# A streaming-encoder block on one Trainium2 core: weight sums made from four loads and a step ahead, gates and boundary loads of the mixer moved by a product

## The chip, the cores and the metric

The kernel runs on one core of a Trainium2 chip. Its engines run side by side, each with its own queue of instructions: PE (TensorE: matmuls), DVE (VectorE: element work and scans), ACT (ScalarE: copies with conversion, activations), POOL (GpSimd, here mostly issuing stores) and SP (SyncE, issuing loads). The metric is the device time of one execution in microseconds (us), lower is better.

## The reference

The block works on x of 1024 rows by 1024 columns, in float32:

```python
x <- LN1(alpha*x + 0.5*FFN1(x))        # FFN(x) = (silu(x @ w_gate) * (x @ w_up)) @ w_down, 1024 -> 4096 -> 1024
z = x @ w_in[l]                        # q, k, v (512 columns each), lru input and its gate (512 each), 8 forget logits
x <- LN2(alpha*x + W_out [FoX(x) ; RG-LRU(x)])
x <- LN3(alpha*x + 0.5*FFN2(x))
```

FoX is causal attention with 8 heads of 64, whose scores get cumulated log-sigmoids of the forget logits. RG-LRU is a causal convolution over four steps, two sigmoid gates from 64 x 64 block matrices, and a linear recurrence along the rows; its result is multiplied by a gelu of the gate columns.

## The kernel before

**Operands.** Each float32 matmul is made of three on PE (`mm3`, L165 to L167): the operands are split into a high part (a cast to fp32r on ACT) and a low part (a subtraction on DVE), and hi x hi, lo x hi and hi x lo are added. Most large products are also done by a scheme that needs seven block products in place of eight (Strassen's, in Winograd's form): each operand is cut into four blocks "11", "12", "21", "22", and sums of blocks (for the weights "t1" to "t4") are operands too. Everywhere the seven products go in the order of `UNIT_ORDER`: "11", "21", "t2", "t1", "t3", "22", "t4". One product is 12 matmuls of 128 x 512.

**Stages.** In order of time: FFN1's gate and up products (to about 600 us), FFN1's down product, the mixer's input products `mixer_in`, `attention` (from about 1180 us), FFN2's gate and up (from about 1400 us), FFN2's down.

**FFN1's gate and up, and `prepare`.** `gate_up` goes through 16 pairs of column blocks, and each pair through a `Matrix` of gate and one of up, seven products each. Its own weights come as `raw`, and become operands by casts on ACT (L385) and subtractions on DVE (L386, L391). The results are copied by ACT (L690, L696, L700) and added by DVE (L703, L706); `silu` is L718. Beside this, `prepare` makes operands that are wanted later (of w_in, and the first ones of FFN2) and stores them to `wq_d`, `wv_d` and other DRAM tiles. It is a generator: `advance()` lets it do one step behind a product of a `Matrix`, 12 times a pair. It loads blocks of 128 x 256 ("aux", L276, by SP) into a pool of four buffers; `keep` (L282 cast on ACT, L283 low part on DVE, L284 store issued by POOL) makes one operand of a block, `less` (L287, DVE) subtracts two blocks in place, and `drop` gives up blocks and asks for as many new ones. A half unit is the seven operands of one half of the rows: it takes seven steps and, in the kernel before, six loads, since the blocks "22" and "12" come twice.

Between 150 and 200 us `mixer_consts` loads small constants and computes from them on ACT (L911, L912).

**The mixer.** `lru_and_qk(c)`, for c from 0 to 3, is one group of 128 channels of the recurrence: a `unit` of seven products for the LRU's input and gate columns, then a `unit` for q and k. A `unit` has two banks of PSUM's s part, `total` (products "11", "t2", "t3", "t4") and `z` ("t1", "22"), and an a bank for "21". What else is to be done stands in a table `then`, whose numbers 1 to 7 are the products it follows: convolution (L970, L972), `gates` (the split of u in L974, L975, two pairs of gate matmuls into a banks, then the recurrence L998 to L1010 and L1013), `out` (L1019 to L1022), `store` of q and k (L1227 on ACT, L1228 on DVE, stores by POOL). L1179 is the addition that is last to read `z`.

**Into attention.** In the last unit, `load_first` asks for head 0's q, kh and kl, `load_rows` for four rows of W_out, and `split_row` splits one (L157 on ACT, L158 on DVE); three more splits come behind the unit. In `attention`, `load` asks for the other operands of a head; `probs` makes the scores of 128 rows (L1329, L1330 on PE into an s tile, L1335 on DVE, L1336 on ACT), and `piece` a tile of the recurrence's part of the output product, with the splits of W_out.

**What sets the order.** A tile scheduler puts out each engine's queue: it follows the order of the program as priorities, the dependences between tiles, the buffers of the pools and `issue_after`. So a changed line can move other instructions too.

Of the kernel before, what the change touches and what calls it, by code (L numbers as in the profile page):

```python
# [13 lines left out]
ALU = mybir.AluOpType  # L14
# [47 lines left out]
class Block:  # L62
# [202 lines left out]
    def prepare(self, jobs, wsp, ap):  # L265
# [20 lines left out]
        def less(x, y):  # L286
            v.tensor_tensor(x, x, y, ALU.subtract)  # L287
# [10 lines left out]
        for blocks, to in jobs:  # L298
# [757 lines left out]
    def load_qk(self, h):  # L1056

        nc, b = self.nc, h % 2
        mine = slice(64 * b, 64 * b + 64)
        for j in range(2):  # L1060
            rows = slice(64 * j, 64 * j + 64)
            for n, src in (("q", self.q_d[h // 2, j]), ("kh", self.k_d[h // 2, 0]), ("kl", self.k_d[h // 2, 1])):
                self.row_load = nc.sync.dma_start(f32(self.heads[n][rows, b, :]), src[mine, :])

    def mixer_in(self, w_out, vw, vp, wp):
# [7 lines left out]
        with self.tc.tile_pool(name="lru_t", bufs=1, reuse_waits="tile") as tp, \  # L1073
# [80 lines left out]
            def unit(c0, c1, c3, then):  # L1154

                def done(n):
                    for g in then.get(n, []):
                        g()

                total = self.s_tile()[:, 0, :]  # L1160
                product(total, "11")
                nc.scalar.copy(c0, total)
                done(1)
                two = self.a_tile()
                product(two, "12")
                v.tensor_tensor(c0, two, c0, ALU.add)
                done(2)
                product(total, "s2", False)
                nc.scalar.copy(c1, total)
                done(3)  # L1170
                z = self.s_tile()[:, 0, :]
                product(z, "s1")
                nc.scalar.copy(c3, z)
                done(4)
                product(total, "s3", False)
                v.tensor_tensor(c3, total, c3, ALU.add)
                done(5)
                product(z, "s4", False)
                v.tensor_tensor(c1, z, c1, ALU.add)  # L1179
                done(6)  # L1180
                product(total, "22", False)
                then[7](total)
# [4 lines left out]
            def lru_and_qk(c, lru_then, qk_then):  # L1187
# [30 lines left out]
                then = {2: [first_conv], 4: [lambda: gates(0)], 6: [lambda: self.gelu_twice(g[:, 0, :], tmp), lambda: out(0)], 7: second_conv}  # L1218
# [5 lines left out]
                def store(n, half, src):  # L1224
# [11 lines left out]
                unit(r[:, 0, :], r[:, 1, :], r[:, 2, :], then)  # L1236
# [27 lines left out]
            w_rows = []  # L1264

            def load_first():
# [362 lines left out]
```

## Time and profile before

| | us |
|---|---|
| median of three runs | 2334.14 (2330.5 to 2335.61) |
| the profiled execution: its own time | 2331.18 |
| the profiled execution: its span | 2329.2 |
| busy in the span: PE / DVE / ACT / POOL | 2290.3 / 1704.9 / 1063.3 / 310.3 |

A busy PE is not PE at its peak: matmuls overlap, so that one row of 0.39 us follows another after 0.23 us. How much PE gets done in a stretch is therefore seen best in the number of its matmuls, and a slower clock in the distance from one start to the next. In a row of a timeline the columns are start, duration, engine, line, operation, out<-in, shapes, and in brackets the idle time before it with what ended it.

### The profile page before, as it was taken

To read this page: it belongs to the slowest core of one execution; us is meant where nothing else is said; L and a number is where in the kernel's file an instruction comes from. 1 tells how busy PE (TensorE), PEld (TensorE's weight loads), DVE (VectorE), ACT (ScalarE), POOL (GpSimd) and SP (SyncE) were. 2 spreads that over 40 slices of the span, in tenths; PEclk is the share of its full clock that TensorE was granted. 3 is DMA by queue.
4 is the path that set the end of the run, shared out by engine and by line. 5 is a ranking of instruction groups with operands and counts; after the bars stand their busy time and mean duration, and the time that the engine had idled before them with its cause. 6 is when DMAs were issued, how large, how long until landed. Compare 5 with 4: busy or idle time off the path is not lost.

```text
span 2329.2 us, 29518 instructions
## 1 busy us (share of the span) xinstructions
PE 2290.3 (98%) x10609; PEld 1896.2 (81%) x10609; DVE 1704.9 (73%) x2745; ACT 1063.3 (46%) x1767; POOL 310.3 (13%) x505
## 2 busy tenths in 40 slices
PE   9999999999999999999989999999999999999998
PEld 7878878787888888988778888888888888888887
DVE  8867777777558779876767999565656565577886
ACT  6444444444334335354556855434343333344342
POOL 0142223232100001111124210000000000000000
PEclk9999999999999999999999999999999999999999
DMA  4565666666276443457676844232323232564542
GB/s 154 195 213 197 222 208 228 208 215 214 105 263 242 140 146 139 152 177 243 211 246 202 241 149 141 86 118 86 118 89 124 94 119 86 188 245 172 181 143 73
DMA packets 221201, 394.44 MB, mean 169 GB/s; under 512 B 14256, under 2 KB 123120, under 8 KB 221056
## 3 DMA queue, kind: packets, MB, share of 16 engines
q1 hardware_dynamic: 184352, 268.50, 35.9%
q0 software_dynamic: 36704, 124.07, 13.6%
q8 instruction: 83, 1.36, 0.2%
q14 instruction: 62, 0.51, 0.1%
HBM read 264.56 MB, written 127.96 MB: 169 GB/s over the span
## 4 chain that ended last, share of the span: by engine, by line
PE 72%; issue 7%; DVE 3%; ACT 2%; DMA 2%; POOL 1%; DVEq 0%; POOLq 0%; ACTq 0%; SPq 0%
PE x L167 6%; PE x L165 6%; PE x L166 6%; PE a L166 6%; PE a L167 6%; PE a L165 6%; PE b L165 5%; PE b L166 5%; PE b L167 5%; PE s L166 5%; PE s L167 5%; PE s L165 5%; PE a L1371 1%; PE a L1350 1%; POOL wq_d L284 1%
## 5 line engine op out<-in xcount | busy, mean ns | idle before, releaser
L385 ACT CAST ws<-t 128x512 fp32r<-128x512 f32 x240 | 147.7, 622 | 311.7 <-PE b L166 139.4
L386 DVE TENSOR_TENSOR ws<-t,ws 128x512 fp32r<-128x512 f32 x240 | 164.2, 686 | 59.5 <-ACT ws L385 35.5
L165 PE MATMUL x<-As,ws 128*128 128x512 f32 x504 | 197.7, 392 | 5.0 <-ACT row L696 4.7
L165 PE MATMUL b<-As,ws 128*128 128x512 f32 x512 | 199.8, 390 | 0.7 <-ACT As L421 0.5
L166 PE MATMUL a<-ws,ws 128*128 128x512 f32 x512 | 199.7, 390 | 0.6 <-DVE ws L817 0.6
L165 PE MATMUL a<-ws,ws 128*128 128x512 f32 x512 | 199.2, 390 | 0.4 <-ACT row L709 0.4
L167 PE MATMUL a<-ws,ws 128*128 128x512 f32 x512 | 199.4, 389 | 0.0
L166 PE MATMUL b<-As,ws 128*128 128x512 f32 x512 | 199.4, 389 | 0.0
L167 PE MATMUL b<-As,ws 128*128 128x512 f32 x512 | 199.2, 389 | 0.0
L167 PE MATMUL x<-A,ws 128*128 128x512 f32 x496 | 194.4, 392 | 4.9 <-DVE ws L386 4.7
L167 PE MATMUL x<-As,ws 128*128 128x512 f32 x504 | 197.1, 391 | 0.0
L166 PE MATMUL x<-As,ws 128*128 128x512 f32 x504 | 197.0, 391 | 0.0
L165 PE MATMUL x<-A,ws 128*128 128x512 f32 x496 | 194.3, 392 | 2.0 <-ACT ws L385 1.2
L166 PE MATMUL x<-A,ws 128*128 128x512 f32 x496 | 193.1, 389 | 0.0
L814 ACT CAST ws<-raw 128x1024 fp32r<-128x1024 f32 x112 | 117.5, 1050 | 160.9 <-PE a L166 82.3
L385 ACT CAST ws<-raw 128x512 fp32r<-128x512 f32 x180 | 110.4, 621 | 172.5 <-PE x L166 136.2
L386 DVE TENSOR_TENSOR ws<-raw,ws 128x512 fp32r<-128x512 f32 x180 | 123.1, 687 | 85.2 <-ACT ws L385 74.3
L744 POOL DMA_DIRECT2D h_d<-row x96 | 69.5, 725 | 858.1 <-DVE row L738 846.0
L817 DVE TENSOR_TENSOR ws<-raw,ws 128x1024 fp32r<-128x1024 f32 x112 | 136.6, 1220 | 47.2 <-ACT ws L814 46.7
L165 PE MATMUL s<-ws,ws 128*128 128x512 f32 x384 | 149.5, 389 | 0.0
L167 PE MATMUL s<-ws,ws 128*128 128x512 f32 x384 | 149.4, 389 | 0.0
L166 PE MATMUL s<-ws,ws 128*128 128x512 f32 x384 | 149.4, 389 | 0.0
(326 smaller groups left out, 5421.7 us busy)
## 6 DMA issues: line engine op xcount, KB each, us to landing
raw<-h_d SPq DMA_DIRECT2D x56, 1024.0 KB, 5.4
h_d<-row POOLq DMA_DIRECT2D x96, 512.0 KB, 3.5
wd<-in_ffn_w_down_dram SPq DMA_DIRECT2D x32, 1024.0 KB, 7.6
raw<-in_ffn_w_gate_dram SPq DMA_DIRECT2D x30, 1024.0 KB, 5.2
raw<-in_ffn_w_up_dram SPq DMA_DIRECT2D x30, 1024.0 KB, 5.2
wq_d<-ws POOLq DMA_DIRECT2D x112, 256.0 KB, 3.8
wq<-wq_d SPq DMA_DIRECT2D x56, 512.0 KB, 4.1
aux<-in_w_in_dram SPq DMA_DIRECT2D x112, 128.0 KB, 3.3
```

What stands on the lines that cost most here:

```text
L165: mm(out, ah, bh, start=first, stop=False, skip_group_check=goes_on)
L166: mm(out, ah, bl, start=False, stop=False, skip_group_check=goes_on)
L167: mm(out, al, bh, start=False, stop=last, skip_group_check=goes_on)
L284: nc.gpsimd.dma_start(to, f32(t).rearrange("p l k f -> p l (k f)"))
L385: nc.scalar.copy(hi, src)
L386: v.tensor_tensor(lo, src, f32(hi), ALU.subtract)
L744: nc.gpsimd.dma_start(d[:, 2 * n:2 * n + 2], t.rearrange("p (r t) -> p r t", r=2))
L814: cast = nc.scalar.copy(hi, src)
L817: self.mark = v.tensor_tensor(lo, src, f32(hi), ALU.subtract)
L1350: nc.tensor.transpose(pa[:, (j % 4) * P:(j % 4 + 1) * P], p[:, j * P:(j + 1) * P], self.ident)
L1371: mm(pv[:, ps], vt[:, j, :], pts[h, qt][j // 4][l][:, j % 4, ps], start=j == 0 and l == 0, stop=j == last and l == 1)
```

## The change

`prepare` loads four blocks for a half unit instead of six and keeps all four until they have been used: `less` gets a place for its result, and every sum is made a step before it is kept, in the place of a block that is done with. The order in which operands are kept becomes 11, t1, 22, t3, t2, 21, t4 (before: 11, t1, 22, t2, 21, t4, t3); each still goes to its own place in DRAM.

In `unit` the seven steps get the names of `UNIT_ORDER`, and so do the tables `then`. The gates of the first half come after "t3" (before: after the product with s1, "t1"), those of the second half after "t2" (before: after "21"). The last unit has `total` in an a bank instead of an s bank. Head 0's q and kh are asked for behind "11" and kl and the cumulated sums behind "21" of the last unit, where before q, kh and kl came behind "21" and the sums in `attention`. Other heads' loads go by operand: q twice, kh twice, kl twice, then the sums.

```diff
-        def less(x, y):
-            v.tensor_tensor(x, x, y, ALU.subtract)
+        def less(to, x, y):
+            v.tensor_tensor(to, x, y, ALU.subtract)
...
-            a, b = ready[0:2]
+            a, b, c, d = ready
             keep(to["11"], a)
-            less(b, a)
-            drop()
+            less(a, b, a)
             yield
-            keep(to["t1"], b)
+            keep(to["t1"], a)
             yield
-            c = ready[1]
             keep(to["22"], c)
-            less(c, b)
-            drop()
+            less(b, c, b)
+            yield
+            keep(to["t3"], b)
+            less(c, c, a)
+            drop(2)
             yield
             keep(to["t2"], c)
             yield
-            a = ready[1]
-            keep(to["21"], a)
-            less(a, c)
+            keep(to["21"], d)
+            less(d, d, c)
             drop()
             yield
-            keep(to["t4"], a)
+            keep(to["t4"], d)
             drop()
-            a, b = ready[0:2]
-            less(a, b)
-            yield
-            keep(to["t3"], a)
-            drop(2)
             yield
...
-            blocks = [view[:, k, c] for k, c in ((up, c0), (up, c1), (down, c1), (down, c0), (down, c1), (up, c1))]
+            blocks = [view[:, k, c] for k, c in ((up, c0), (up, c1), (down, c1), (down, c0))]
...
-                total = self.s_tile()[:, 0, :]
+                total = self.a_tile() if last else self.s_tile()[:, 0, :]
...
-                then = {2: [first_conv], 4: [lambda: gates(0)], 6: [lambda: self.gelu_twice(g[:, 0, :], tmp), lambda: out(0)], 7: second_conv}
+                then = {"21": [first_conv], "t3": [lambda: gates(0)], "22": [lambda: self.gelu_twice(g[:, 0, :], tmp), lambda: out(0)], "t4": second_conv}
...
-                then = {2: [lambda: store(0, 0, r[:, 0, :]), lambda: gates(1), lambda: out(1)], 5: [lambda: store(1, 1, r[:, 2, :])],
-                        6: [lambda: store(1, 0, r[:, 1, :])], 7: lambda total: store(0, 1, total)}
+                then = {"21": [lambda: store(0, 0, r[:, 0, :])], "t2": [lambda: gates(1), lambda: out(1)], "t3": [lambda: store(1, 1, r[:, 2, :])],
+                        "22": [lambda: store(1, 0, r[:, 1, :])], "t4": lambda total: store(0, 1, total)}
...
+            def open_heads(names, k):
+                for l, n in enumerate(names):
+                    self.heads[n] = vp.tile([P, 2, T], F32 if n == "cum" else F32R, tag=f"w{k + l}", name=self.nm(n))
                 with self.tc.issue_after(self.row_load.ins):
-                    self.load_qk(0)
+                    for n in names:
+                        self.load_head(0, n)
...
-                           {3: [self.forget]} if c == 0 else {2: [load_first], 3: [load_rows], 6: [split_row]} if c == 3 else {})
+                           {"t2": [self.forget]} if c == 0 else
+                           {"11": [lambda: open_heads(("q", "kh"), 0)], "21": [lambda: open_heads(("kl", "cum"), 2)], "t2": [load_rows], "22": [split_row]} if c == 3 else {})
```

How the queues move is seen in the order of the instructions. In the kernel with the change the lines up to some 1050 are 5 lower (L381 is L386 before, L698 is L703, L906 and L907 are L911 and L912, L685 is L690, L704 is L709), those of `attention` 14 higher.

DVE, a half unit of `prepare` and the beginning of the next pair (`aux` is a block or a sum of blocks, `ws` a kept operand), before:

```order
L283 TENSOR_TENSOR ws_548_2719<-aux_541_2662,ws_548_2719 128x256
L287 TENSOR_TENSOR aux_543_2681<-aux_543_2681,aux_541_2662 128x256
L283 TENSOR_TENSOR ws_551_2755<-aux_543_2681,ws_551_2755 128x256
L283 TENSOR_TENSOR ws_552_2772<-aux_545_2701,ws_552_2772 128x256
L287 TENSOR_TENSOR aux_545_2701<-aux_545_2701,aux_543_2681 128x256
L283 TENSOR_TENSOR ws_555_2793<-aux_545_2701,ws_555_2793 128x256
L283 TENSOR_TENSOR ws_556_2810<-aux_546_2703,ws_556_2810 128x256
L287 TENSOR_TENSOR aux_546_2703<-aux_546_2703,aux_545_2701 128x256
L283 TENSOR_TENSOR ws_558_2830<-aux_546_2703,ws_558_2830 128x256
L703 TENSOR_TENSOR row_493_2485<-x_547_2705,row_492_2484 128x512
L287 TENSOR_TENSOR aux_549_2724<-aux_549_2724,aux_553_2777 128x256
L386 TENSOR_TENSOR ws_568_2846<-raw_566_2843,ws_567_2845 128x512
```

and now:

```order
L283 TENSOR_TENSOR ws_534_2691<-aux_525_2616,ws_534_2691 128x256
L287 TENSOR_TENSOR aux_525_2616<-aux_526_2618,aux_525_2616 128x256
L283 TENSOR_TENSOR ws_536_2725<-aux_525_2616,ws_536_2725 128x256
L287 TENSOR_TENSOR aux_526_2618<-aux_530_2656,aux_526_2618 128x256
L283 TENSOR_TENSOR ws_537_2742<-aux_530_2656,ws_537_2742 128x256
L287 TENSOR_TENSOR aux_530_2656<-aux_530_2656,aux_525_2616 128x256
L283 TENSOR_TENSOR ws_539_2761<-aux_526_2618,ws_539_2761 128x256
L283 TENSOR_TENSOR ws_542_2783<-aux_530_2656,ws_542_2783 128x256
L283 TENSOR_TENSOR ws_543_2800<-aux_532_2675,ws_543_2800 128x256
L287 TENSOR_TENSOR aux_532_2675<-aux_532_2675,aux_530_2656 128x256
L381 TENSOR_TENSOR ws_553_2816<-raw_551_2813,ws_552_2815 128x512
L698 TENSOR_TENSOR row_480_2459<-x_533_2677,row_479_2458 128x512
```

The sum with a reloaded block (L287 with aux_549 and aux_553) is gone from ahead of the next pair's first low part, and that low part (L386, now L381) has gone ahead of the addition L703 (now L698).

ACT around the mixer's constants (`lp` and `vecs` are the constants, `x` a product's bank), before:

```order
L282 CAST ws_313_1452<-aux_262_1313 128x256
L911 ACTIVATE lp_315_1497<-vecs_1488 128x4
L690 COPY row_272_1360<-x_329_1628 128x512
L912 ACT_TABLE_LOAD
L912 ACTIVATE lp_315_1497<-lp_315_1497 128x4
L282 CAST ws_320_1546<-aux_264_1332 128x256
```

and now:

```order
L906 ACTIVATE lp_312_1491<-vecs_1482 128x4
L282 CAST ws_311_1448<-aux_258_1291 128x256
L907 ACT_TABLE_LOAD
L907 ACTIVATE lp_312_1491<-lp_312_1491 128x4
L685 COPY row_270_1356<-x_326_1622 128x512
L282 CAST ws_317_1540<-aux_258_1291 128x256
```

The copy of a product (L690, now L685) stood ahead of the table load and now stands behind it and behind one more cast.

PE from the mixer into attention (`s` and `a` are banks, `wq` the last unit's operands, `w` the splits of W_out, `mix` the recurrence's output), before:

```order
L166 MATMUL s_1808_10134<-xT_1542_8210,wq_1828_10232 128x512
L167 MATMUL s_1808_10134<-xT_1541_8209,wq_1828_10232 128x512
L1329 MATMUL s_1855_10364<-kh_1821_10201,q_1820_10200 128x512
L1330 MATMUL s_1855_10364<-kl_1822_10202,q_1820_10200 128x512
L1329 MATMUL s_1855_10364<-kh_1821_10201,q_1820_10200 128x384
L1330 MATMUL s_1855_10364<-kl_1822_10202,q_1820_10200 128x384
L165 MATMUL a_1858_10378<-w_1833_10285,mix_1596_8869 128x512
```

and now:

```order
L1343 MATMUL s_1815_10284<-kh_1771_10071,q_1770_10070 128x512
L1344 MATMUL s_1815_10284<-kl_1776_10098,q_1770_10070 128x512
L1343 MATMUL s_1815_10284<-kh_1771_10071,q_1770_10070 128x384
L1344 MATMUL s_1815_10284<-kl_1776_10098,q_1770_10070 128x384
L165 MATMUL a_1818_10298<-w_1793_10206,mix_1556_8789 128x512
L166 MATMUL a_1818_10298<-w_1794_10207,mix_1556_8789 128x512
L167 MATMUL a_1818_10298<-w_1793_10206,mix_1557_8790 128x512
L165 MATMUL a_1818_10298<-w_1797_10228,mix_1620_9180 128x512
L165 MATMUL a_1768_10054<-xT_1501_8129,wq_1788_10153 128x512
```

The last product (from `xT`) stood ahead of the second scores; now the second scores and the first four matmuls of a piece, which read splits of W_out, stand ahead of it.

More of the change, by code (lines that the diff above doesn't have):

```diff
@@ L1152, in product, with unit, one, two @@
                     self.mm3(x, (w[:, 0, k, :], w[:, 1, k, :]), x_op(name, k), new and k == 0, k == 3, not new)
[L1154 to L1158, printed above, removed]
-                total = self.s_tile()[:, 0, :]
[L1161 to L1182, printed above, removed]
+            def unit(c0, c1, c3, then, last=False):
+                total = self.a_tile() if last else self.s_tile()[:, 0, :]
+                bank = {}
+                def one():
+                    product(total, "11")
+                    nc.scalar.copy(c0, total)
+                def two():
+                    x = self.a_tile()
+                    product(x, "12")
+                    v.tensor_tensor(c0, x, c0, ALU.add)
+                def six():
+                    product(total, "s2", False)
+                    nc.scalar.copy(c1, total)
+                def five():
+                    bank["z"] = self.s_tile()[:, 0, :]
+                    product(bank["z"], "s1")
+                    nc.scalar.copy(c3, bank["z"])
+                def seven():
+                    product(total, "s3", False)
+                    v.tensor_tensor(c3, total, c3, ALU.add)
+                def three():
+                    product(bank["z"], "s4", False)
+                    v.tensor_tensor(c1, bank["z"], c1, ALU.add)
+                def four():
+                    product(total, "22", False)
+                steps = {"11": one, "21": two, "t2": six, "t1": five, "t3": seven, "22": three, "t4": four}
+                for n in UNIT_ORDER:
+                    steps[n]()
+                    if n == "t4":
+                        then[n](total)
+                    else:
+                        for g in then.get(n, []):
+                            g()
@@ L1262, in s4 @@
                     parts("s4", j, quarters(j)[0][1])
[L1264 to L1268 removed]
+            w_rows, self.heads = [], {}
+            def open_heads(names, k):
+                for l, n in enumerate(names):
+                    self.heads[n] = vp.tile([P, 2, T], F32 if n == "cum" else F32R, tag=f"w{k + l}", name=self.nm(n))
                 with self.tc.issue_after(self.row_load.ins):
[L1270 removed]
+                    for n in names:
+                        self.load_head(0, n)
             def load_rows():
```

28 lines of the change are left out of this document (15 added, 13 removed).

## The prediction

> **What bounds the kernel now.** I read the page first, then a table by stage, the waits of PE, and the timeline around the longest of them.
>
> ```profile
> span 2329.2 us, 29518 instructions
> PE 2290.3 (98%) x10609; PEld 1896.2 (81%) x10609; DVE 1704.9 (73%) x2745; ACT 1063.3 (46%) x1767; POOL 310.3 (13%) x505
> ```
>
> PE is busy 98% of the span, and the change takes no matmul away. So all it can win are PE's stops and the slow matmuls after them. Busy time hides the second kind; counts of matmuls in a window (the first bracket behind its length) show both:
>
> ```profile
> 150.00:200.00 50.00, 46.28 (x191) 37.38 (x190) 37.40 (x83) 23.37 (x43) 21.51 (x34) 0.93 0.61 195
> 200.00:600.00 400.00, 393.19 (x1714) 319.76 (x1713) 301.45 (x543) 190.67 (x368) 111.81 (x161) 1.00 0.63 214
> 1050.00:1150.00 100.00, 97.75 (x425) 78.94 (x424) 68.27 (x111) 49.95 (x74) 15.27 (x26) 1.00 0.71 232
> 1150.00:1200.00 50.00, 43.06 (x168) 34.04 (x167) 33.77 (x50) 28.52 (x39) 8.26 (x14) 0.90 0.84 281
> 1500.00:1900.00 400.00, 400.00 (x1767) 331.20 (x1766) 247.87 (x366) 155.17 (x253) 27.26 (x40) 1.00 0.29 102
> ```
>
> The last row, FFN2 without stops, gives the full pace: 400 / 1767 = 0.2264 us a matmul. Against it 200 to 600 (FFN1 gate/up) is short of 53 matmuls, 12.0 us; 150 to 200 (the mixer's constants) of 30, 6.8 us; 1050 to 1150 (most of the mixer) of 17, 3.8 us; 1150 to 1200 (mixer into attention) of 53, 12.0 us. PE's waits name the stops:
>
> ```profile
> PE x L167 <- DVE ws L386: 4.7, 9, 1.0
> PE x L165 <- ACT row L696: 4.7, 2, 3.5
> PE s L1329 <- DVE ev L1228: 3.1, 1, 3.1
> PE s L1329 <- DVE raw L1179: 3.0, 1, 3.0
> PE a L165 <- ACT ua L974: 2.2, 5, 0.5
> PE a L166 <- DVE ue L975: 2.0, 5, 0.8
> ```
>
> Row 1 is the FFN1 pairs' boundaries, row 2 the constants (3.5) and one boundary, rows 3 and 4 the step into attention, rows 5 and 6 the gates: ten stops, 4.2 us. The change touches all four places.
>
> **Part 1: four loads and an earlier order in prepare.** One boundary, and the group that paces it (groups of 200 to 600):
>
> ```profile
> 294.67 0.41 ACT L282 CAST ws<-aux 128x256 fp32r<-128x256 f32 x1 [1.02 <-issue]
> 294.98 1.14 ACT L385 CAST ws<-raw 128x512 fp32r<-128x512 f32 x2
> 295.45 0.68 DVE L703 TENSOR_TENSOR row<-x,row 128x512 f32<-128x512 f32 x1
> 296.60 1.29 DVE L386 TENSOR_TENSOR ws<-raw,ws 128x512 fp32r<-128x512 f32 x2
> 297.34 0.50 PE L167 MATMUL x<-A,ws 128*128 128x512 f32 x1 [0.95 <-DVE ws L386]
> 409.48 0.50 PE L165 MATMUL x<-As,ws 128*128 128x512 f32 x1 [1.26 <-ACT row L696]
> L287 DVE TENSOR_TENSOR aux<-aux,aux 128x256 f32<-128x256 f32 x67 | 28.2, 424 | 26.5 <-DMA aux<-in_w_in_dram 20.3 <-DMA aux<-in_ffn_w_gate_dram 4.7 <-DMA aux<-in_ffn_w_up_dram 0.2
> ```
>
> DVE idles 25.2 us ahead of L287 for reloaded blocks; the half unit then ends late, its last cast (294.67) stands ahead of the next pair's first (294.98), and L386 comes 0.95 us late, behind L703 as well. In the change each block is asked for at least four steps before its sum, and a difference that is kept was made a step earlier. The order also puts L386 ahead of L703 (0.68). The seven casts, seven low parts, four differences and seven stores of a half unit stay; two of its six loads go, 40 of 128 KB in all, so nothing is added on any engine. At a boundary L386 comes 0.68 earlier by the order and up to 1.0 earlier by the cast that was late, against stops of 0.4 to 1.0. I take 9 of 12.0 us: some boundaries also wait for L385's own input. Bounds: 2 (only L703's place counts at the nine stops, and a later step of the chain is late instead) and 12.0.
>
> **Part 2: the constants.** Their DMAs are untouched, but the order of ACT around them moves.
>
> ```profile
> 160.37 0.21 ACT L911 ACTIVATE lp<-vecs 128x4 f32<-128x4 f32 x1 [4.45 <-DMA vecs<-in_lru_lambda_dram]
> 160.48 0.57 ACT L690 COPY row<-x 128x512 f32<-128x512 f32 x1
> 161.07 1.28 ACT L912 ACT_TABLE_LOAD   x1
> 169.06 0.71 ACT L282 CAST ws<-aux 128x256 fp32r<-128x256 f32 x2 [2.43 <-DVE aux L287]
> 170.30 0.79 PE L165 MATMUL x<-As,ws 128*128 128x512 f32 x1 [3.45 <-ACT row L696]
> 170.90 0.63 PE L166 MATMUL x<-As,ws 128*128 128x512 f32 x1
> 171.32 0.63 PE L167 MATMUL x<-As,ws 128*128 128x512 f32 x1
> ```
>
> Before, the copy that PE waits for (L690) comes right behind L911, and PE stops 0.26 us there; the large stop, 3.45, is at L696, where an L282 waits 2.43 us for L287. Behind that stop matmuls follow at 0.42 us (170.90 to 171.32) instead of 0.2264. Now L690's copy stands behind one L282 (0.4) and L912's table load and activation: 0.4 + 1.28 + 0.21 = 1.9 us more, so the first stop becomes about 2.2. The second loses most of the 2.43 that the L282 waited and keeps casts ahead of it: about 1.4 at full pace, none if PE was slow in between. The slow stretch now costs 6.8 - 3.45 - 0.26 = 3.1. With one stretch behind the first stop and no second stop: 2.2 + 3.1 = 5.3, to which I add 0.2 for half a chance of a rest of the second: 5.5, a gain of 1.3. With no slow stretch 2.2 + 1.4 = 3.6, a gain of 3.2; with one behind both stops, 9.8, a loss of 3.
>
> **Part 3: gates a product later.**
>
> ```profile
> 1168.05 0.51 PE L166 MATMUL a<-ue,hi 128*128 128x512 f32 x1 [0.33 <-DVE ue L975]
> 1168.82 0.69 ACT L998 ACTIVATE t<-a,vecs 128x512 f32<-128x512 f32 x1 [0.76 <-PE a L167]
> ```
>
> A product is 12 matmuls, 2.72 us. The first half's gates get it whole, and their stops (one of five pairs, 1.1 us) go. The second half's (eight of ten stops) stand behind the first half's recurrence, which starts with L998 when the first half's gates are done, 2.72 later too. So the distance between the halves stays, and of a second pair's stops I take off about a third, for the rows of the unit's stores that no longer stand between. Stops cost 4.2 plus some 0.17 each in the restart (at 409.48 PE is 1.42 behind its pace for 1.26 of idle), 5.9 in all; I take 2.4, between 0 and 5.9.
>
> **Part 4: into attention.** Timeline, PE first, then DVE and ACT:
>
> ```profile
> 1178.59 0.39 PE L167 MATMUL s<-As,wq 128*128 128x512 f32 x1
> 1181.93 0.50 PE L1329 MATMUL s<-kh,q 128*128 128x512 f32 x1 [2.95 <-DVE raw L1179]
> 1190.57 0.80 PE L1329 MATMUL s<-kh,q 128*128 128x512 f32 x1 [3.11 <-DVE ev L1228]
> 1197.03 0.40 PE L1329 MATMUL s<-kh,q 128*128 128x512 f32 x1
> 1181.19 0.68 DVE L1179 TENSOR_TENSOR raw<-s,raw 128x512 f32<-128x512 f32 x1
> 1185.11 4.80 DVE L158 TENSOR_TENSOR w<-wout,w 128x1024 fp32r<-128x1024 f32 x4
> 1189.84 0.68 DVE L1228 SCALAR_TENSOR_TENSOR ev<-s,ev 128x512 fp32r<-128x512 f32 x1
> 1190.44 1.21 DVE L1335 CUSTOM_DVE_ANT_0 p<-s,cum 128x1024 f32<-128x1024 f32 x1
> 1181.91 0.63 ACT L1227 ACTIVATE ev<-raw 128x512 fp32r<-128x512 f32 x1 [1.36 <-DVE raw L1179]
> 1182.44 3.88 ACT L157 CAST w<-wout 128x1024 fp32r<-128x1024 f32 x4
> ```
>
> Two banks hold `total` and `z` and are freed late: z by L1179 at 1181.87 (stop A), total by the last L1228 at 1190.52, behind the four L158 (stop B).
> Stop A stays. The bank that total leaves now takes the first scores; the second scores wait for z. From L998's start (1168.82) z comes free in 13.05 us, for 10.0 of which PE has work (to 1178.82). In the change PE has 43 matmuls behind the first of the second half's gates (three of the other gate, 36 of three products, four of scores), 9.74 us, and DVE has one L1228 (0.6 from start to start) less ahead of z: 12.4 - 9.7 = 2.7, a gain of 0.3.
> Stop B changes its cause. From z's release to the third scores it is now 1197.03 - 1181.87 = 15.2 us. In the change: L1227 0.63, the first L157 about 1.0, the first L158 1.2, together 2.8, the first piece's four matmuls to 3.7, the last product 2.72, to 6.4; L1227 0.6 and L1228 0.7, by then past the four L158 (0.63 + 1.0 + 4.8 = 6.4), L1335 1.21, 0.2 to start: 9.1. At half pace the product takes 1.4 more, 10.5. Gain 4.7 (slow) to 6.1; I take the slow end, since 2.95 of idle is followed by a slow stretch and 2.7 is nearer to that than to 1.26 (409.48, no slow row behind it). With stop A: 5.0.
> Price of the earlier loads: head 0's q, kh and then kl, cum are now asked for after the last unit's first two products.
>
> ```profile
> kh<-k_d SPq DMA_DIRECT2D x16, 256.0 KB, 6.0
> ```
>
> Asked for behind the first product, 2.7 to 5 us into the unit, kh lands at 11 at the latest, and the first scores, 54 matmuls into the unit, want it at 12.2: about 1.2 in hand, so nothing is charged. If kh were 2 late, PE would stop for 1 more.
>
> **Sum.** 9 + 1.3 + 2.4 + 5.0 = 17.7 us off the profiled execution, 2331.18 (its span of 2329.2 and 2.0 around it): 2313.5. The median of the three runs, 2334.14, is 3.0 above it, so on the scale of the median 2316.5; I predict **2316 us**.
>
> A rule bears on the largest doubt. The Trainium skill, "TensorE: Matmul & The Clock Gate", section "HAM oscillation", says that PE must not idle for more than about 3.4 us if its clock is to stay up. This trace differs: the slow stretch begins behind 2.95 of idle. By the page neither the 2.2 nor the 2.7 us stop would have one.
>
> **Rivals.**
> - *The clock stays up* at stops of 2.2 to 2.7. For: 1.26 has no slow stretch. Against: 2.95 has. Part 2 gives 3.2 and part 4 6.4, with 9 and 2.4: 21.0 off, 2313 on the scale of the median.
> - *All boundary and gate stops vanish*: 12.0 and 5.9 instead of 9 and 2.4, 24.2 off, 2310. For: each stop is under 1.3, and a product is 2.72. Against: DVE's order behind the recurrence.
> - *The boundaries stay*: the chain cast, subtraction, cast of the next sum is itself what paces a half unit, not the load; only 2 of 9 is won, 10.7 off, 2323.4. For: L282 waits for L287 (2.43 at 169.06). Against: 25.2 us of idle on DVE name the DMA.
> - *It does nothing*: the loads in flight are four deep as before, and another transfer is late at the same boundaries; the gains at attention are eaten by kh. 2334.
> - *Slower: z comes late at every channel group.* With the gates 2.72 later, the recurrence of the second half ends later, and the z bank of the next group's first unit is freed behind it. PE has about 1.2 us in hand there by my count of matmuls against DVE's chain; it decides once the chain slips by 4.2 (1.2 and a stop of 2.95). Then each of three group boundaries costs a stop and a slow stretch like stop A's, about 6: 18, against 10.3 of parts 1 and 2: 7.7 slower, 2342. For: at the last group stop A is this. Against: DVE is busy 68 of 100 us between 1050 and 1150, and a slip of one product leaves 1.5 missing.
>
> **How the numbers follow.** Forecast 0.48, clock up 0.13, all stops gone 0.10, boundaries stay 0.12, nothing 0.07, slower 0.10. A difference under 0.2% (4.7 us) can't be told from none. Faster: 0.48 + 0.13 + 0.10 + 0.12 = 0.83; same 0.07; slower 0.10. The forecast's own range is 2311 to 2322, from the bounds of parts 2 to 4; with the rivals on the fast side and the boundaries that stay, 2306 to 2327, which leaves out the last two cases.
>
> **What would show it.** Part 1: 200 to 600 with about 1755 matmuls, L287's idle for DMA near 0. Part 2: a stop of about 2.2 at L690's line and none of 3.45. Part 3: no first-half gate stop, second-half ones under 0.8. Part 4: a stop near 2.7 for z, then one for L158's first result, and third scores about 10 us after z's release. Wrong would be: stops at the starts of units in the mixer, or PE waiting for kh or q.

## The result and the profile after

The changed kernel takes 2313.41 us (median of four runs, 2312.88 to 2314.6); the kernel before took 2334.72 (four runs, 2330.5 to 2335.61). The ratio is 0.9913, with a 95% interval of 0.9896 to 0.9930. The two profiled executions took 2313.64 and 2331.18, 17.5 us apart. Forecast were 2316 for the median, in a range of 2306 to 2327, and 17.7 us off the profiled execution. The kernel before, run again beside the experiments, had medians of 2330.3 to 2331.4, so 17 to 18 us is nearer to what the change is worth than the 21 between these two medians.

The page of the kernel after, the same two rows as before:

```profile
span 2311.6 us, 29444 instructions
PE 2282.1 (99%) x10609; PEld 1897.2 (82%) x10609; DVE 1704.5 (74%) x2745; ACT 1063.7 (46%) x1767; POOL 310.1 (13%) x505
```

The work is the same; PE is busy 8 us less in a span 17.6 us shorter. Some 5 us of that are matmuls at the slow pace: by the distances between their starts they cost 6.9 us before, in three stretches, and 2.0 after, in one. The stretches that were short of matmuls, in the table by stage (PE's matmuls in the first bracket):

```profile
150.00:200.00 50.00, 47.44 (x208) 38.66 (x207) 37.87 (x84) 24.81 (x46) 21.27 (x34) 1.00 0.61 197
200.00:600.00 400.00, 399.27 (x1761) 330.25 (x1760) 308.85 (x553) 194.99 (x373) 111.17 (x160) 1.00 0.59 202
1050.00:1150.00 100.00, 98.65 (x432) 80.33 (x431) 70.78 (x115) 54.40 (x80) 14.64 (x22) 1.00 0.69 219
```

From 200 to 600 us 1761 matmuls are done where 1714 were, 6 short of full pace. PE's waits after:

```profile
PE s L1343 <- DVE raw L1182: 4.0, 1, 4.0
PE a L166 <- DVE ue L970: 1.6, 3, 0.5
PE x L165 <- ACT row L685: 1.5, 1, 1.5
PE a L166 <- DVE w L158: 1.1, 1, 1.1
PE x L165 <- ACT row L691: 1.1, 1, 1.1
PE x L167 <- DVE ws L381: 0.7, 1, 0.7
```

The boundaries' row has gone from 4.7 us in nine stops to 0.7 in one (last row), the constants' 3.5 to 1.5 and 1.1. The stop for z (first row) has grown from 3.0 to 4.0.

Where the time went is read best from the start of the same instruction in both timelines:

| mark | before | after | difference |
|---|---|---|---|
| a pair's silu ahead of the constants | 121.03 | 122.42 | +1.4 |
| the silu behind them | 205.33 | 201.05 | -4.3 |
| FFN1's last pair, first silu | 629.87 | 615.68 | -14.2 |
| first matmul of the mixer's last unit | 1159.68 | 1142.72 | -17.0 |
| third scores of head 0 | 1197.03 | 1178.60 | -18.4 |
| last matmul | 2320.69 | 2302.07 | -18.6 |
| end of the span | 2329.2 | 2311.6 | -17.6 |

So the constants gave 5.7 us (1.4 of it at a pair's boundary ahead of them), the boundaries 9.9, the mixer up to its last unit 2.8, the last unit and the step into attention 1.5. At the head 1.4 and at the tail 1.0 were lost; neither was followed up. At these marks PE has done equally many matmuls in both, within one, but for the silu behind the constants: there it has done 887 before and 882 after. Counted by PE's work, 1.1 us of the constants' gain therefore belong to the boundaries, 4.6 and some 11.

The last two gains come from one pair of executions, and the one of before is slow there. From the mixer's first product to the third scores it took 186.6 us; four other profiles in which the mixer is as before took 183.6, 183.6, 185.3 and 186.1 (six buffers, loads by POOL, prepare alone, low part ahead, all below). With the whole change the stretch took 182.7, in variants that leave the mixer as changed 182.5 to 183.1. So some 2 us on the mean, and not 4.3, is what gates, banks and head 0's loads are worth together.

### The profile page after: what moved, and what is told of

Its sections match the earlier page's. It is cut to its first block, busy times and chain, and to the rows that moved or that the text cites. A ratio compares the mean times of both kernels' runs of the same rounds, so it can differ in the third digit from the quotient of the medians.

```text
span 2311.6 us, 29444 instructions
## 1 busy us (share of the span) xinstructions
PE 2282.1 (99%) x10609; PEld 1897.2 (82%) x10609; DVE 1704.5 (74%) x2745; ACT 1063.7 (46%) x1767; POOL 310.1 (13%) x505
## 4 chain that ended last, share of the span: by engine, by line
PE 87%; DVE 5%; issue 3%; ACT 2%; DMA 2%; POOL 1%; SPq 0%; DVEq 0%; POOLq 0%; ACTq 0%
PE x L165 9%; PE x L167 9%; PE x L166 9%; PE b L166 7%; PE b L165 7%; PE b L167 7%; PE a L165 6%; PE a L166 6%; PE a L167 6%; PE s L165 5%; PE s L167 5%; PE s L166 5%; PE a L1385 1%; PE a L1364 1%; PE a L1090 1%
## 5 line engine op out<-in xcount | busy, mean ns | idle before, releaser
L381 DVE TENSOR_TENSOR ws<-t,ws 128x512 fp32r<-128x512 f32 x240 | 163.8, 686 | 69.9 <-ACT ws L380 36.6
L809 ACT CAST ws<-raw 128x1024 fp32r<-128x1024 f32 x112 | 117.4, 1050 | 160.6 <-PE a L166 81.0
L381 DVE TENSOR_TENSOR ws<-raw,ws 128x512 fp32r<-128x512 f32 x180 | 123.1, 687 | 91.9 <-ACT ws L380 74.3
```

Of the source, the lines that this page charges most:

```text
L381: v.tensor_tensor(lo, src, f32(hi), ALU.subtract)
L809: cast = nc.scalar.copy(hi, src)
```

## The experiments

The theory at their start: the prepare's part is worth most, because reloaded blocks came late; the gates give what the changed distance gives; at the step into attention the bank of the last total is the gain and the later gates the price. Rivals were that the order on DVE, not the loads, made the boundary stops; that the number of loads on SP did; and that the mixer's parts pay nothing. The kernel before was run beside each group: its medians there were 2331.37, 2330.34 and 2330.8 us.

### Prepare alone, and everything but prepare

The kernel before with only the first two hunks of the diff (prepare and its list of blocks):

```diff
-            blocks = [view[:, k, c] for k, c in ((up, c0), (up, c1), (down, c1), (down, c0), (down, c1), (up, c1))]
+            blocks = [view[:, k, c] for k, c in ((up, c0), (up, c1), (down, c1), (down, c0))]
```

> The kernel before with the new prepare alone (four loads, sums a step ahead); unit, gates, banks and head 0's loads as before. Theory (the FFN1 half of the change is prepare's alone): the stretch from 150 to 600 us gives what it gave in the whole change, about 5 us at the constants and 10.8 us at the pairs' boundaries, so about 2334.7 - 16 = 2318.5; stops at L386's line 1 instead of 9, no stop of 3.45. Rival (the constants' part comes from other moved work, prepare's is only the boundaries): about 2324, with a stop over 3 us left near 166 us.

Measured: 2315.34 us (2314.25 to 2316.09), ratio 0.9928 (0.9909 to 0.9948). The stretch from 200 to 600 us does 1762 matmuls, as in the whole change, and the silu behind the constants comes 4.0 us earlier than before (201.37). The theory's number, 2318.5, was 3 too high, as it started from 2334.7; its gain of 16 us came.

The changed kernel with the old prepare is the reverse of that:

> The changed kernel with the old prepare (six loads, sums in the step of their keep); gates, banks and head 0's loads as changed. Theory (the parts add up): the mixer's and attention's parts are about 2.2 and 1.9 us by the two traces, so 4 to 5 us under the kernel before, about 2330; nine or so stops at the pairs' boundaries again. Rival (the mixer's parts only pay because FFN1 ends earlier or its stores land earlier): no more than 1 us under the kernel before, 2334.

Measured: 2330.00 us (2326.31 to 2332.3), ratio 0.9992 (0.9981 to 1.0003): by the total not to be told from no change. By the timeline the mixer and attention's part is there: against the kernel before it is 6.0 us behind at FFN1's last pair (635.91) and 1.6 behind at the third scores (1198.58), 4.5 won, while this execution's boundaries lost more than the profiled one of before. Four profiles of kernels with the old prepare did 1714, 1692, 1697 and 1726 matmuls there; with the new one they did 1760 to 1765. Both totals add up: 16.0 and 1.4 are 17.4, near the 17.5 of the profiled pair. So prepare is worth some 16 us, and everything else in the change 1.4 to 1.9 (2315.34 against 2313.41).

### Which part of prepare

Six buffers for the old prepare, so that a block can be asked for two earlier (one buffer of gu_ws given up):

```diff
-            blk.pool("gu_ws", 15) as wsp, blk.pool("aux", 4) as ap, blk.banks() as bank, ExitStack() as inner:
+            blk.pool("gu_ws", 14) as wsp, blk.pool("aux", 6) as ap, blk.banks() as bank, ExitStack() as inner:
...
-        for _ in range(4):
+        for _ in range(6):
             fetch()
```

> The kernel before, six loads a half unit and the old order of sums, with six buffers for blocks instead of four, so that each load is asked for two steps earlier; one of gu_ws's 15 buffers is given up for the room. Theory (the loads were late): DVE's idle time for aux loads ahead of L287 between 200 and 600 falls from 25 to under 8 us, the stops at the boundaries mostly go, 6 to 9 us faster, about 2327. Rival (the order of sums and keeps is what counts, a sum in the step of its keep and L703 ahead of L386): the idle time for the DMA goes, but the stops stay at 4 us or more and the time within 2 us of the kernel before, 2333 to 2335.

Measured: 2331.14 us (2327.68 to 2335.72), ratio 1.0000 (0.9988 to 1.0012). Neither half of the theory's reading came: the group of differences (200 to 600) waits as long for the DMA, and PE's stops at the boundaries are fewer and longer.

```profile
L287 DVE TENSOR_TENSOR aux<-aux,aux 128x256 f32<-128x256 f32 x67 | 28.0, 424 | 29.6 <-DMA aux<-in_w_in_dram 21.9 <-DMA aux<-in_ffn_w_up_dram 5.0 <-DMA aux<-in_ffn_w_gate_dram 1.6
PE x L167 <- DVE ws L386: 5.1, 6, 1.7
```

More depth in this form doesn't help. As one buffer of another pool is missing too, it doesn't clear the loads altogether.

Next, the changed kernel with two more loads a half unit that nothing reads (in `fetch`; the list of blocks has them behind each four, and they go to scratch in DRAM):

```diff
+            while isinstance(src, tuple):
+                nc.sync.dma_start(spare[next(turn) % 8], src[0])
+                src = next(specs, None)
```

> The changed kernel with two more loads of 128 KB a half unit on SP, as many bytes and issues as before, of blocks that nothing reads (they go to scratch in DRAM), so that sums and keeps stay as changed. Theory (how many loads must pass SP in the part of a pair in which it isn't waiting for a weight block's buffer is what made the sums late): half or more of the 10.8 us between 200 and 600 us is lost again, about 2320, with DVE waiting over 15 us for aux loads. Rival (the order of sums and keeps is what counts): within 2 us of the changed kernel, 2313 to 2316, L386's (now one line lower than L381) stops as few as there.

Measured: 2315.21 us (2314.39 to 2316.79), ratio 0.9935 (0.9917 to 0.9954). Its group of differences and its row of the table by stage:

```profile
L292 DVE TENSOR_TENSOR aux<-aux,aux 128x256 f32<-128x256 f32 x69 | 29.2, 423 | 16.5 <-DMA aux<-in_w_in_dram 11.9 <-DMA aux<-in_ffn_w_gate_dram 2.4 <-DMA aux<-in_ffn_w_up_dram 1.1
200.00:600.00 400.00, 399.29 (x1760) 329.82 (x1759) 307.70 (x553) 194.50 (x372) 111.39 (x161) 1.00 0.62 212
```

The same group in the changed kernel:

```profile
L287 DVE TENSOR_TENSOR aux<-aux,aux 128x256 f32<-128x256 f32 x68 | 28.8, 423 | 8.9 <-DMA aux<-in_w_in_dram 7.4
```

DVE waits 15.4 us for blocks, twice the 7.4 of the changed kernel, and PE loses nothing by it. So the number of loads that pass SP is not the cause, and DVE's idle time for a DMA was the wrong measure of it: it costs only where the chain behind it ends late.

The block loads of the kernel before issued by POOL:

```diff
-                nc.sync.dma_start(t, src)
+                nc.gpsimd.dma_start(t, src)
```

> The kernel before with the blocks' loads issued by POOL instead of SP; six loads, old order of sums. Theory (SP's queue holds them behind weight loads that wait for their buffers): DVE's wait for aux loads between 200 and 600 falls from 25 to under 10 us and 5 us or more are won there, 2325 or less. Rival (the order of sums, or POOL's own stores ahead of them): the stops at the pairs' boundaries stay, 2329 to 2336.

Measured: 2357.08 us (2354.98 to 2358.42), ratio 1.0112 (1.0096 to 1.0129), 27 us slower. It made a stop of its own:

```profile
PE x L165 <- ACT ws L385: 23.5, 12, 3.8
```

The casts of FFN1's own weights came late in twelve places. DVE's wait for blocks fell only from 25.2 to 20.6 us, where the theory asked for under 10. What held the casts wasn't followed, so this run says nothing about SP.

Then the order on DVE at the boundaries, by one added dependence in each kernel. In the changed one the next pair's first low part has to stay behind the last t3 addition, as before:

```diff
             w["11"] = parts(b11)
+            if steps and pair > 1:
+                self.issue_behind(self.last_lo, self.last_seven)
```

> The changed kernel in which, in FFN1's gate and up, the first low part of each pair has to stand behind the last pair's t3 addition on DVE (L698 there), as it stood before; loads, sums and keeps as changed. Theory (the place of that low part on DVE makes most of the boundary stops): at the pairs' boundaries some eight stops of about 0.4 to 0.7 come back, 4 us or more, 2318 to 2322. Rival (the addition comes early enough now that nothing in the half unit is late, so the order there is free): under 2 us lost, 2313 to 2315.5.

Measured: 2312.14 us (2310.5 to 2313.29), ratio 0.9923 (0.9910 to 0.9937). 1763 matmuls from 200 to 600 us: the order is worth nothing there. In the kernel before, the reverse (`self.issue_behind(self.last_seven, self.last_lo)`, once a pair):

> The kernel before (six loads, old order of sums and keeps) in which the last pair's t3 addition has to stand behind the first low part of the next pair on DVE, as the change has it at its boundaries. Theory (that order makes most of the gain at the boundaries): 4 to 7 us faster than the kernel before, stops of L386 falling from 4.7 to under 2 in all. Rival (the half unit's own lateness makes the stops): no more than 2 us faster.

Measured: 2328.58 us (2326.68 to 2331.08), ratio 0.9993 (0.9984 to 1.0002). Its waits and its row by stage:

```profile
PE x L165 <- ACT ws L385: 2.0, 3, 1.0
PE x L167 <- DVE ws L386: 1.7, 4, 0.8
200.00:600.00 400.00, 394.71 (x1725) 322.21 (x1724) 302.35 (x544) 191.77 (x370) 111.38 (x161) 1.00 0.63 214
```

L386's stops fall from 4.7 us in nine to 1.7 in four, those for L385 grow from 1.2 to 2.0. 1725 matmuls are 11 more than before, 2.5 us, and far from 1761. The total, 2.2 us lower, can't be told from no change.

What fits most of these is how long the prepare of a pair takes in one piece. All its twelve steps run between the pair's first silu and the next pair's first cast. ACT at one boundary, before (the last cast, at 294.67, and L385 behind it stand in the prediction):

```profile
279.00 1.06 ACT L718 ACTIVATE row<-row 128x1024 f32<-128x1024 f32 x1 [1.66 <-DVE row L706]
...
286.26 0.41 ACT L282 CAST ws<-aux 128x256 fp32r<-128x256 f32 x1 [1.48 <-DVE aux L287]
288.37 0.41 ACT L282 CAST ws<-aux 128x256 fp32r<-128x256 f32 x1 [1.70 <-DVE aux L287]
```

and after:

```profile
272.11 1.06 ACT L713 ACTIVATE row<-row 128x1024 f32<-128x1024 f32 x1 [0.54 <-DVE row L701]
...
285.94 0.71 ACT L282 CAST ws<-aux 128x256 fp32r<-128x256 f32 x2 [0.28 <-ACT ws L282]
286.56 1.14 ACT L380 CAST ws<-raw 128x512 fp32r<-128x512 f32 x2
```

The next pair's cast starts 16.0 us after the silu before (279.00 to 294.98) and 14.5 after (272.11 to 286.56). Over the ten pairs from 190 to 560 us the last of the twelve casts starts on the mean

| kernel | us after the silu |
|---|---|
| before | 16.5 |
| before, low part ahead | 16.5 |
| before, six buffers | 15.1 (12.9 to 17.8) |
| changed | 14.5 |
| changed, low part behind | 14.5 |
| changed, two idle loads | 14.6 |

14.5 is early enough that hardly a boundary waits, whatever the order there; 16.5 is not, and the order then saves some 2 us of 12. Six buffers don't fit this: two of that kernel's boundaries stop for L386 behind pieces of 14.9 and 15.0 us (0.93 and 0.45), and it is 41 matmuls short. Its missing buffer of weights may be why; that wasn't separated.

The new prepare takes 2 us out of this piece. What in it does so is not shown. Three things came together and none was tried alone: no block is loaded a second time, a sum is made a step before it is kept, and t3 is kept ahead of t2. The waits of ACT's casts from 200 to 600 us speak for the second. Before and after:

```profile
L282 ACT CAST ws<-aux 128x256 fp32r<-128x256 f32 x121 | 46.5, 404 | 81.5 <-DVE aux L287 39.3 <-issue 14.0 <-DMA aux<-in_w_in_dram 10.7
L282 ACT CAST ws<-aux 128x256 fp32r<-128x256 f32 x120 | 45.6, 405 | 51.7 <-DVE aux L287 17.2 <-PE x L166 9.9 <-issue 7.6
```

A cast waited for a sum for 39.3 us before and 17.2 after. With two idle loads it is 14.6, though DVE waits twice as long for its blocks there; with six buffers it is 24.9. With a step between a sum and its cast, a block that comes late need not hold the cast.

### The gates alone

```diff
-                then = {2: [first_conv], 4: [lambda: gates(0)], 6:
+                then = {2: [first_conv], 5: [lambda: gates(0)], 6:
...
-                then = {2: [lambda: store(0, 0, r[:, 0, :]), lambda: gates(1), lambda: out(1)], 5:
+                then = {2: [lambda: store(0, 0, r[:, 0, :])], 3: [lambda: gates(1), lambda: out(1)], 5:
```

> The kernel before with both gates one product later and nothing else. Theory (the distance from the first gates to the second stays, the last unit's chain on DVE gets later against PE): the ten gate stops of 4.2 us fall to about 2, 2.2 us won, and the stop for z at the step into attention grows from 2.95 to about 4, 1 lost: 1 us faster in all, about 2333.5. Rival 1 (a product more is enough for all gates): 5 to 6 us faster, 2329, no stop over 0.2 us at the gates. Rival 2 (z comes late at each group): stops at the first product of each LRU unit, 5 us or more slower, 2340.

Measured: 2328.70 us (2325.86 to 2329.52), ratio 0.9985 (0.9976 to 0.9995), 2.7 us faster. The second half's gates still stop PE (1.6 us in three), and the stop for z grows to 3.6. By the timeline 4.9 us are won between the mixer's first product and the third scores (181.7 against 186.6), more than the theory's 1.2. Behind the second stop, of 3.5 us, PE goes on at full pace here; before, it was slow behind it:

```profile
1190.51 0.50 PE L1329 MATMUL s<-kh,q 128*128 128x512 f32 x1 [3.48 <-DVE ev L1228]
1190.85 0.39 PE L1330 MATMUL s<-kl,q 128*128 128x512 f32 x1
```

The slow rows behind that stop before add up to 2.6 us above the full pace; take them away and 2.3 are left for the gates. Either way the gates alone give as much as gates, banks and loads together did above (2330.00 by the total, 182.5 by the timeline).

### The last unit: total's bank, the last gates, the loads, z's bank

The changed kernel with total back in an s bank (`unit(...)` without its `c == 3`):

> The changed kernel with the last unit's total back in an s bank. Theory (that bank was worth the second stop): both stops of about 3 to 4 us stand there again, for z and for L158's row behind it, the third scores come 2 to 4 us later than in the changed kernel, 2316. Rival (the changed stop of 4.0 plus 2.5 of later waits costs as much as the two stops of before): within 1 us, 2313.5.

Measured: 2314.68 us (2309.62 to 2316.3), ratio 0.9927 (0.9908 to 0.9946): not to be told from the changed kernel. Its waits:

```profile
PE s L1343 <- DVE raw L1182: 4.5, 1, 4.5
PE s L1343 <- DVE ev L1240: 2.0, 1, 2.0
```

The rival held: the bank moves the stop more than it shortens it.

The last unit's second gates back behind "21":

```diff
-                then = {"21": [lambda: store(0, 0, r[:, 0, :])], "t2": [lambda: gates(1), lambda: out(1)], "t3":
+                second = [lambda: gates(1), lambda: out(1)]
+                then = {"21": [lambda: store(0, 0, r[:, 0, :])] + (second if c == 3 else []), "t2": [] if c == 3 else second, "t3":
```

> The changed kernel with the last unit's second gates back behind "21", the others a product later. Theory (the later gates make the last unit's chain on DVE later against PE, which made the stop for z 4.0 instead of 2.7): the stop for z falls to between 1.5 and 2.7, the last gates' stops of 0.3 and 0.5 come back, the third scores come 1 to 2 us earlier, 2312. Rival (the chain is later for another reason, the stores that DVE now does between): the stop stays at 3.5 or more and the time at 2313.4 or above.

Measured: 2314.66 us (2311.71 to 2317.28), ratio 0.9931 (0.9912 to 0.9949). The stop for z falls from 4.0 to 3.2, less than the theory asked, and the gates' own stop grows to 1.1. Nothing is won, which fits the reading that PE waits for the work on DVE and ACT between the last gates and the softmax, in one place or another.

Head 0's four loads all behind "21":

```diff
-"11": [lambda: open_heads(("q", "kh"), 0)], "21": [lambda: open_heads(("kl", "cum"), 2)]
+"21": [lambda: open_heads(("q", "kh"), 0), lambda: open_heads(("kl", "cum"), 2)]
```

> The changed kernel with all of head 0's loads behind "21" of the last unit, as q, kh and kl were before. Theory (the first scores want kh 54 matmuls, 12.2 us, into that unit, and kh then lands at 13 to 15): a stop of 1 to 3 us for a DMA ahead of the first scores, most of it taken back by a shorter stop for z, 2314. Rival (kh lands in time anyway): no stop for kh or q, 2313.4.

Measured: 2313.23 us (2312.24 to 2313.6), ratio 0.9928 (0.9914 to 0.9942). No wait for kh or q; the first scores run without a stop, ahead of the same 4.0 for z:

```profile
1156.82 0.39 PE L1343 MATMUL s<-kh,q 128*128 128x512 f32 x1
1164.64 0.80 PE L1343 MATMUL s<-kh,q 128*128 128x512 f32 x1 [4.03 <-DVE raw L1182]
```

So asking for them earlier buys nothing, and costs nothing.

Last, z in an a bank too, and the pieces of the output product held behind the last product:

```diff
-                    bank["z"] = self.s_tile()[:, 0, :]
+                    bank["z"] = self.a_tile() if last else self.s_tile()[:, 0, :]
...
-                self.down_tile(i, lru_tiles, (d,), True)
+                with self.tc.issue_after(self.last_mm.ins):
+                    self.down_tile(i, lru_tiles, (d,), True)
```

(`last_mm` is the last matmul of the last `product`.)

> The changed kernel with the last unit's z in an a bank too, and the pieces of the output product behind the last unit's last product on PE. Theory (what PE waits for from 1162 to 1179 us is DVE's chain from the last gates to the W_out splits and the first softmax row; banks and the order on PE only decide where it waits): the stop of 4.0 for z goes, PE works 2.7 us further (the last product) and waits there for the first split, and the third scores come about 3 us earlier, because the fourth split no longer waits for the last product: 2310.5. Rival (the chain is as long and ends in the same third scores): within 1 us, 2313.4.

Measured: 2309.55 us (2308.26 to 2310.78, five runs), ratio 0.9913 (0.9900 to 0.9927) against the kernel before beside it. Its slowest run is under the fastest of the changed kernel (2312.88), and its median is the lowest of the versions: 3.9 us under the changed kernel and 2.6 under the nearest, low part behind, run beside it. PE and DVE around the step:

```profile
1165.55 0.47 PE L165 MATMUL a<-xT,wq 128*128 128x512 f32 x1 [3.23 <-DVE raw L1182]
1173.62 0.47 PE L1343 MATMUL s<-kh,q 128*128 128x512 f32 x1 [0.75 <-DVE m L1349]
1167.10 4.63 DVE L158 TENSOR_TENSOR w<-wout,w 128x1024 fp32r<-128x1024 f32 x4 [0.24 <-ACT w L157]
```

Third scores at 1173.62 against 1178.60. The stop didn't go to the first split, as the theory had it: it stands ahead of the last product. The profile names L1182, which ends at 1165.47; the operands of that product, a load issued at 1154.06, land at 1165.41. The times are too near to tell which of the two PE waited for; by the program the last product goes into the bank of `total` and neither reads nor writes z, which speaks for the load.

## Why the prediction was right, point by point

**Part 1**, 9 us forecast, 9.9 measured (some 11 by PE's work). The row read (L287 waiting for aux loads) led to the right place and size, but two of its terms fell. The 0.68 us for L386 ahead of L703 is worth nothing in the changed kernel, and 2.5 us in all in the kernel before; and DVE's 25 us of waiting is no price, since 15.4 us of it do no harm. What counts is the length of the piece from a pair's silu to the next pair's first cast, which I had not measured: 16.5 us on the mean before, 14.5 after. The prediction named both the late reloads and the sums made a step earlier as what shortens it, and put the price on the reloads; which of the two counts is not shown, and ACT's casts speak for the sums. The forecast of about 1755 matmuls in that stretch stood at 1761. The rival "the boundaries stay" fell by its number; its premise, that the chain of casts and sums sets the pace and not the load, is not refuted.

**Part 2**, 1.3 us forecast, 4.2 measured, from the silu at 154.56 before (154.51 after) to that at 205.33 (201.05). The stops were 1.5 and 1.1 instead of 2.2 and a rest; the step that failed is the slow stretch of 3.1 us that I kept behind the first stop. There was none: the clock's column for 150 to 200 us went from 0.93 to 1.00. In this part the rival "the clock stays up", with a gain of 3.2, was nearer. That was luck in part: in the run with total back in an s bank, an edit to the last unit alone, the stop at this place was 2.1 and a slow stretch of 1.6 us followed it.

**Part 3**, 2.4 us forecast, 2.8 measured up to the last unit; alone 2.7 by the totals. The distance between first and second gates stays, as argued: 2.0 us of gate stops are left of 4.2. The slower rival, z late at every group, never showed.

**Part 4**, 5.0 us forecast, 1.5 measured from the start of the last unit, and by the totals nothing that could be told. Two steps failed. The first is that stop A would shrink to 2.7. From the first tanh to z's release the chain takes 12.2 us, as worked out (12.4), but the tanh no longer starts when its gate is done. ACT, after:

```profile
1151.22 1.28 ACT L980 ACT_TABLE_LOAD   x1
1152.51 0.63 ACT L980 ACTIVATE g<-g 128x512 f32<-128x512 f32 x1
1153.05 0.61 ACT L1239 ACTIVATE ev<-raw 128x512 fp32r<-128x512 f32 x1
1153.57 0.57 ACT L1169 COPY raw<-a 128x512 f32<-128x512 f32 x1
1154.04 0.69 ACT L993 ACTIVATE t<-a,vecs 128x512 f32<-128x512 f32 x1
```

Before, the same tanh (L998) came 0.76 us after ACT had run out of work; now four rows stand ahead of it without a gap, a table load among them, and it comes about 1.5 us after its gate, whose last matmul starts at 1152.14 and takes 0.39. 1.5 + 12.2 - 9.7 = 4.0, the stop that is there.

The second is the 9.1 to 10.5 us from z's release to the third scores. They took 12.3 (1166.27 to 1178.60):

```profile
1178.60 0.47 PE L1343 MATMUL s<-kh,q 128*128 128x512 f32 x1 [1.10 <-DVE m L1349]
1168.58 3.49 DVE L158 TENSOR_TENSOR w<-wout,w 128x1024 fp32r<-128x1024 f32 x3
1175.48 1.23 DVE L158 TENSOR_TENSOR w<-wout,w 128x1024 fp32r<-128x1024 f32 x1 [3.41 <-issue]
1176.63 0.69 DVE L1240 SCALAR_TENSOR_TENSOR ev<-a,ev 128x512 fp32r<-128x512 f32 x1
1177.23 1.21 DVE L1349 CUSTOM_DVE_ANT_0 p<-s,cum 128x1024 f32<-128x1024 f32 x1
```

I had the four splits done before the last product; the fourth starts 3.4 us late, when that product is over, and the first softmax row stands behind it. The trace names nothing that the fourth waited for. Splits and operands of products share a pool, and in the last experiment, with the product earlier, the four run without a gap. The 1.2 us that I held in hand for kh were not needed.

That the whole came out so near has to do with errors that cancel: the constants gave 2.9 more, the mixer 0.4 more and attention 3.5 less than forecast, and the boundary ahead of the constants (1.4) and the gain at the others (0.9) stand against what was lost at head and tail (2.4). That the profiled execution of before was slow in the mixer and attention helped too.

## What to carry to other kernels

Don't price a wait on an engine that isn't the bottleneck by its length: find the piece of work that has to be done between two marks of the bottleneck, measure how long it takes, and compare it with the room. Where a step is moved, look also at what then stands ahead of its consumer in the consumer's own queue, a table load above all. Compare two timelines only at marks with the same work ahead of them, and with more than one execution of each. A bank moved away from a stop only helps if the chain that frees the next thing is shorter; here total's bank alone gave nothing that could be told, while z's bank, with PE's own last product ahead of the matmuls that wait, gave 2.6 to 3.9 us.

## What the runs showed of the hardware

Whether PE is slow behind a stop isn't decided by the length of the stop. In the profile of the gates alone full pace follows 3.48 us (above). In that of total back in an s bank rows 0.43 us apart come behind a stop of 2.1:

```profile
163.66 0.63 PE L167 MATMUL x<-As,ws 128*128 128x512 f32 x1
164.09 0.63 PE L165 MATMUL x<-As,ws 128*128 128x512 f32 x1
164.52 0.63 PE L166 MATMUL x<-As,ws 128*128 128x512 f32 x1
```

They begin 1.3 us after PE has started again (162.37). Shorter stops had one too: 1.68 us with the gates alone (slow from 297.81), 1.29 with the loads by POOL (from 602.08) and 0.90, behind one of 0.65, with the old prepare (from 220.22). Most slow stretches cost between 1.4 and 2.8 us in these profiles, so at each stop of some 1 us or more such a sum hangs on something that the runs don't show. The Trainium skill, "TensorE: Matmul & The Clock Gate", section "HAM oscillation", puts the bound at idle gaps of about 3.4 us; the runs have slow stretches below it and none behind 3.48.
